# A hybrid layer's merge, output projection and Strassen quarters: whole row tiles, four banks at a time, one quarter summed on TensorE

## The chip, the cores and the metric

The kernel runs on one core of one Trainium2 chip. Its engines are TensorE (PE, with PEld for its weight loads), VectorE (DVE), ScalarE (ACT), GpSimd (POOL) and SyncE (SP, which only issues DMAs here). The metric is the device time of one execution in microseconds. Before the change it is 1715.71 us, the median of 3 runs (1714.04 to 1716.68).

## The reference

One layer of a hybrid decoder, 1024 tokens of width 1024 behind 16 meta tokens, all in float32:

```python
xn = rmsnorm(h, norm_mix)
q, k, v, u, g_att, g_ssm = jnp.split(xn @ w_in, offs, axis=-1)
attn = sliding_window_attention(rmsnorm(q), rmsnorm(k), v, attn_sinks)
y = s5_ssm(u, ...)                                   # diagonal complex scan
z = jax.nn.gelu(y)
za, zb = jnp.split(z @ w_glu, 2, axis=-1)
ssm = za * jax.nn.sigmoid(zb)
merged = (jax.nn.sigmoid(g_att) * rmsnorm(attn, attn_branch_norm)
          + jax.nn.sigmoid(g_ssm) * rmsnorm(ssm, ssm_branch_norm))
h = h + merged @ w_out
gate, up = jnp.split(rmsnorm(h, norm_ffn) @ w_ffn_in, 2, axis=-1)
h = h + (jax.nn.silu(gate) * up) @ w_ffn_out
```

## The kernel before

Every large product works on operands in two parts. `split` makes them: ScalarE casts the source to the TensorE format (`hi`), VectorE subtracts that from the source (`lo`), and the product is three passes, hi by hi, lo by hi and hi by lo, so a 128x512 output block over a depth of 1024 is 24 matmuls (`mm3`).

The work comes in stages. First the input projections, the state space scan and attention, up to about 680 us of the profiled execution. Then the scan's output y is made, passed through gelu, transposed, and split into four quarters of z (b11, t3, b21, b22), in the loop over `blk` whose helper is `z_turn`. The product with w_glu is a Strassen scheme of 2x2 quarters: seven products, with the keys "11", "12", "2", "3", "22", "1", "4", need three mixed quarters more, t2 = t3 + b11, t4 = b21 - t2 and t1 = b22 - t2. `mixed` makes those on VectorE. A unit is one such product for a pair of column blocks; its 12 matmuls a key go to PSUM banks named ch, si, th and ex. The first two units, (1,0) and (0,0), run together (`glu_step`), then the others follow.

Behind the gate comes the merge, `merge(h)`, once for each half of the tokens. It turns the sum of squares of ssm (a matmul, `ssq`) into a factor (14 small VectorE instructions), spreads it over partitions (a matmul, `rsb`, copied by ScalarE to `rs`), multiplies the eight blocks of ssm by it (L1055), adds the attention half, read back from DRAM in eight loads of 256 KB into cells `mpa` on SP's queue, and splits the sum into `mt`. The output projection then makes h = x + merged @ w_out in two column halves n and eight row blocks b (banks `wo`, evicted by VectorE in L1140 together with a load of x, `xr`), and norms and transposes h for the feed-forward part, which again is a Strassen product. There too t2, t4 and t1 are mixed, for the first two units (names with `_e`).

SBUF is handed out by pools of tiles. `pool_a` has 8 half tiles of 128 x 4 x 512 (class `Rows` joins two), `pool_x` holds the mixed quarters, `big` the pages, `mp` the cells. PSUM has 8 banks: tags m and s with 2 each, taken in turn, x with 3 and q with 1. The order of instructions on an engine is not that of the source: a scheduler places them by its own estimates, and each engine then runs its queue in order.

## Time and profile before

| | |
|---|---|
| median of 3 runs | 1715.71 us |
| the profiled execution | 1708.9 us, span 1707.1 us |
| PE busy | 1572.0 us, 92% of the span |
| DVE busy | 1262.4 us, 74% |
| ACT busy | 730.5 us, 43% |
| POOL busy | 296.5 us, 17% |
| mean granted clock of TensorE | 0.967 of full speed |

The profiled execution is one run with the profiler on; it is 6.8 us below the median. TensorE works almost without gaps over the whole span, except in a few short stretches. A stretch loses time in two ways: TensorE sits idle, which the timeline shows with the engine that released it, or its granted clock is below 1.00, which is the lower of its two levels for part of the stretch, and each matmul then takes longer though it counts as busy.

### The profile page before, as it was taken

The numbers are of one execution on the slowest core, as the hardware profiler recorded it, in microseconds if no ns is written. First come the engines' busy times: TensorE is split into PE (matmuls) and PEld (weight loads), VectorE is DVE, ScalarE is ACT, GpSimd is POOL, SyncE is SP. The second block draws the span as 40 slices with busy tenths as digits, with TensorE's granted clock in tenths as the row PEclk, the third lists the DMA queues.
The fourth block names the chain that finished last, engine by engine and source line by source line (L and its number), as shares of the span: only waits on it lengthen the run. The fifth ranks groups of instructions, "written<-read, shape, count | busy, mean of one in ns | idle before, by whom it ended". The sixth has DMA issues, their size and how long they took to land. (4 is left out here: it accounts for less than half of the span.)

```text
span 1707.1 us, 22184 instructions
## 1 busy us (share of the span) xinstructions
PE 1572.0 (92%) x7906; PEld 1299.7 (76%) x7906; DVE 1262.4 (74%) x2446; ACT 730.5 (43%) x1435; POOL 296.5 (17%) x233
## 2 busy tenths in 40 slices
PE   7999978989989999889996697999999999799998
PEld 5788868778867788857885585788888888678887
DVE  7779886999994799688756478966655656299763
ACT  4434425878985321554432233533333333243330
POOL 1001313333321000000000000111111112256441
PEclk9999989999999999989998898999999999899999
DMA  6254442011013763711234251323323331485431
GB/s 189 61 129 134 146 142 73 11 41 42 22 50 116 255 207 115 223 44 68 80 99 130 80 191 62 129 94 109 108 80 106 99 120 60 152 324 183 154 111 74
DMA packets 167166, 196.92 MB, mean 115 GB/s; under 512 B 12768, under 2 KB 117216, under 8 KB 166928
## 3 DMA queue, kind: packets, MB, share of 16 engines
q1 hardware_dynamic: 158544, 183.94, 33.2%
q10 hardware_dynamic: 8288, 11.01, 2.0%
q8 instruction: 62, 1.02, 0.3%
q0 software_dynamic: 224, 0.56, 0.1%
q14 instruction: 48, 0.39, 0.1%
HBM read 140.62 MB, written 54.85 MB: 115 GB/s over the span
## 5 line engine op out<-in xcount | busy, mean ns | idle before, releaser
L122 PE MATMUL g<-xn,wh_g 128*128 128x512 f32 x512 | 165.4, 404 | 1.3 <-ACT sg L548 1.2
L814 PE MATMUL ch<-B,A 128*128 128x512 f32 x528 | 126.5, 396 | 9.8 <-ACT B L1360 7.6
L814 PEld LDWEIGHTS ch<-B,A 128*128 128x128 f32 x528 | 100.2, 191 | 33.6 <-ACT B L1360 8.1
L122 PEld LDWEIGHTS g<-xn,wh_g 128*128 128x128 f32 x512 | 97.1, 192 | 24.6 <-ACT sg L548 2.1
L122 PE MATMUL q<-wh_q,xn 128*128 128x256 f32 x512 | 104.3, 291 | 4.2 <-ACT qp L620 4.2
L122 PE MATMUL wo<-wh_o,mt 128*128 128x512 f32 x256 | 84.0, 407 | 22.5 <-DVE h L1140 14.7
L122 PE MATMUL g<-xn,wl_g 128*128 128x512 f32 x256 | 102.6, 401 | 0.0
L818 POOL TENSOR_TENSOR a<-c_e,c_e 128x512 f32<-128x512 f32 x1 | 1.5, 1542 | 571.6 <-DVE c_e L818 571.6
L814 PE MATMUL si<-B,A 128*128 128x512 f32 x396 | 92.7, 389 | 0.0
L122 PE MATMUL u<-xn,wh_u 128*128 128x272 f32 (+2 forms) x384 | 91.7, 332 | 0.0
L122 PEld LDWEIGHTS q<-wh_q,xn 128*128 128x128 f32 x512 | 84.4, 195 | 5.8 <-ACT qp L620 4.6
L814 PEld LDWEIGHTS si<-B,A 128*128 128x128 f32 x396 | 74.3, 188 | 15.7 <-DVE h2o L818 0.3
L1360 ACT CAST A<-rawa 128x1536 fp32r<-128x1536 f32 (+1 forms) x28 | 38.5, 1374 | 96.3 <-issue 44.8
L122 PEld LDWEIGHTS wo<-wh_o,mt 128*128 128x128 f32 x256 | 50.0, 196 | 34.2 <-issue 15.1
L122 PE MATMUL q<-wl_q,xn 128*128 128x256 f32 x256 | 74.2, 290 | 0.0
L818 DVE TENSOR_TENSOR A<-rawa,A 128x1536 fp32r<-128x1536 f32 (+1 forms) x28 | 62.8, 2243 | 12.8 <-ACT A L1360 12.8
L669 ACT ACTIVATE pr<-pr,mn 128x272 f32<-128x272 f32 (+1 forms) x128 | 64.9, 507 | 16.5 <-DVE mn L663 14.0
L818 POOL TENSOR_TENSOR a<-c,c_fg 128x512 f32<-128x512 f32 x10 | 15.9, 1586 | 316.1 <-DVE c L818 211.1
L122 PEld LDWEIGHTS u<-xn,wh_u 128*128 128x128 f32 x384 | 66.1, 196 | 5.5
L818 POOL TENSOR_TENSOR B<-t,B 128x1536 fp32r<-128x1536 f32 (+1 forms) x16 | 60.3, 3781 | 50.5 <-ACT B L1360 50.5
L122 PE MATMUL u<-xn,wl_u 128*128 128x272 f32 (+2 forms) x192 | 63.0, 330 | 0.0
L818 DVE TENSOR_TENSOR h2o<-h2o,ch 128x512 f32<-128x512 f32 x64 | 42.3, 679 | 26.4 <-PE ch L814 24.3
(449 smaller groups left out, 4222.3 us busy)
## 6 DMA issues: line engine op xcount, KB each, us to landing
rawa<-act_d SPq DMA_DIRECT2D x21, 768.0 KB
raw_fg<-in_w_ffn_in_dram SPq DMA_DIRECT2D x20, 512.0 KB
raw_fu<-in_w_ffn_in_dram SPq DMA_DIRECT2D x20, 512.0 KB
rawb<-in_w_ffn_out_dram SPq DMA_DIRECT2D x6, 1536.0 KB
act_d<-a SPq DMA_DIRECT2D x33, 256.0 KB
raw_g<-in_w_in_dram SPq DMA_DIRECT2D x16, 512.0 KB
raw_z<-in_w_glu_dram SPq DMA_DIRECT2D x16, 512.0 KB
act_d<-c_fg SPq DMA_DIRECT2D x30, 256.0 KB
```

What stands on the lines that cost most here:

```text
L122: nc.tensor.matmul(o, lhs(kb, a), rhs(kb, b), start=(kb == 0 and i == 0), stop=(kb == n - 1 and i == 2))
L669: nc.scalar.activation(out=pr[:, h, :n], in_=pr[:, h, :n], func=AF.Exp, scale=-1.0, bias=mn[:, h:h + 1], accum_out=den[:, h:h + 1])
L814: nc.tensor.matmul(o, lhs(kb, a), rhs(kb, b), start=(first and kb == 0 and i == 0), stop=(kb == n - 1 and i == 2), skip_group_check=not first)
L818: eng.tensor_tensor(out=out, in0=in0, in1=in1, op=op)
L1360: nc.scalar.copy(hi, src)
```

## The change

It has six parts. (1) `pool_a` gets 4 whole row tiles of 128 x 8 x 512 in place of 8 halves, and the class `Rows` goes. (2) The quarters of z lie in pairs in such tiles, (b11, t3) and (b21, b22), so one split of 512 columns serves a transposed bank where two of 256 did; of four copies to `ss` per block VectorE makes two instead of three. (3) The first operands of the gate unit (1,0), for keys "11", "12" and "22", are made ahead of the loop over y. (4) The quarter t2 is summed on TensorE: four matmuls by an identity (`one_r`) add the hi and lo parts of t3 and b11 in one bank, ScalarE and VectorE split that bank, and ScalarE copies it out for the two other mixed quarters. In the FFN the sum stands ahead of both first units. (5) The attention half comes in four loads of 1 MB on GpSimd's queue, into tiles of `pool_x` that t2 and t1 leave free, and the merge adds in place in ssm. (6) The output projection's first column half works on four banks at once, one 128-deep slice after the other through all four.

```diff
-    pool_a = front.enter_context(sbuf("pool_a", 8))
+    pool_a = front.enter_context(sbuf("pool_a", 4))
+    one_r = const.tile([P, P], F32R, name="one_r")
+    nc.vector.tensor_copy(one_r, ident)
-    def mm3(o, lhs, rhs, n):
-        for kb in range(n):
+    def mm3(o, lhs, rhs, n, only=None):
+        for kb in range(n) if only is None else [only]:
...
+    def rows_a(name, n=512):
+        return pool_a.tile([P, KB, n], F32R, tag="a", name=name)
...
+    def x_pair(key):
+        t = rows_a(f"X{key}")
+        X[key] = [t[:, 4 * p:4 * p + 4, :] for p in range(2)]
...
-    def mixed(key, a, b, op):
+    def mixed(key, a, b, op, tag="s"):
+        if key == "t2":
+            for k in range(4):
+                pt = bank(f"{key}_{k}", tag)
+                for i, v in enumerate((X[b][0], X[b][1], X[a][0], X[a][1])):
+                    nc.tensor.matmul(pt, one_r, v[:, k, :], start=(i == 0), stop=(i == 3))
+                if k % 2 == 0:
+                    full[k] = page(f"{key}f{k}").rearrange("p (k n) -> p k n", k=2)
+                split(X[key][0][:, k, :], X[key][1][:, k, :], pt)
+                nc.scalar.copy(full[k // 2 * 2][:, k % 2, :], pt)
+            return
         for k in (0, 2):
             t = page(f"{key}f{k}").rearrange("p (k n) -> p k n", k=2)
...
-            if key == "t2":
-                full[k] = t
-                l2 = page(f"{key}l{k}").rearrange("p (k n) -> p k n", k=2)
-                tt_(t, hi, X[b][0][:, k:k + 2, :].bitcast(F32), op)
-                tt_(l2, lo, X[b][1][:, k:k + 2, :].bitcast(F32), op)
-                tt_(t, t, l2, ALU.add)
...
+    two = ((1, 0), (0, 0))
+    a2, ops = {two[0]: glu_raw(*two[0])}, {u: {} for u in two}
+    ops[two[0]] = glu_operands(a2[two[0]], ("11", "12", "22"), "10")
...
-            for h in range(2):
-                dst = [X[keys[h]][p][:, blk % 4].rearrange("p (n t) -> p t n", t=T)[:, 4 * i:4 * i + 4, :]
-                       for p in range(2)]
-                split(dst[0], dst[1], pt.rearrange("p (t n) -> p t n", t=4)[:, :, 64 * h:64 * h + 64])
+            dst = [Z[keys][p].rearrange("p (h k) (n t) -> p k t h n", h=2, t=T)[:, blk % 4, 4 * i:4 * i + 4]
+                   for p in range(2)]
+            split(dst[0], dst[1], pt.rearrange("p (t h n) -> p t h n", t=4, h=2))
...
-                cp_ = nc.vector.tensor_copy if e or ri else nc.scalar.copy
+                cp_ = nc.vector.tensor_copy if e else nc.scalar.copy
...
+        def load_pa(h):
+            pa[h] = [x_tile(f"pa{h}{i}").bitcast(F32) for i in range(2)]
+            for i in range(2):
+                nc.gpsimd.dma_start(out=pa[h][i], in_=pa_d[4 * i:4 * i + 4, :, 512 * h:512 * h + 512]
+                                    .rearrange("f p n -> p f n"))
 
         def merge(h):
             rs = rstd_cols(acc[h], 4, f"ssm{h}", mp, cell(f"rs{h}"))
             for f in range(KB):
                 src = ssm[h, f // 2][:, (f % 2) * 512:(f % 2) * 512 + 512]
-                pa = cell(f"mpa{f}{h}")
-                nc.sync.dma_start(out=pa, in_=pa_d[f][:, 512 * h:512 * h + 512])
                 nc.vector.tensor_tensor(out=src, in0=src, in1=rs, op=ALU.mult)
-                tt_(pa, pa, src, ALU.add)
-                split(mt[h][0][:, f, 0:512], mt[h][1][:, f, 0:512], pa)
+                tt_(src, src, pa[h][f // 4][:, f % 4, :], ALU.add)
+                split(mt[h][0][:, f, 0:512], mt[h][1][:, f, 0:512], src)
...
-                o = bank(f"wo{n}{b}")
-                mm3(o, lambda kb, part: mt[b // 4][part][:, kb, (b % 4) * P:(b % 4 + 1) * P], w, KB)
+                if n == 0 and b % 4 == 0:
+                    wo = [bank(f"wo{n}{b + i}") for i in range(4)]
+                    for kb in range(KB):
+                        for i in range(4):
+                            mm3(wo[i], lambda k, part: mt[b // 4][part][:, k, i * P:i * P + P], w, KB, kb)
+                o = wo[b % 4] if n == 0 else bank(f"wo{n}{b}")
...
         for key in ("t2", "t1", "t4"):
-            x_part(key, pool_a)
+            x_pair(key)
+        mixed("t2", "t3", "b11", ALU.add, "x")
```

The queues change at three places. First VectorE at the merge of the first half of the tokens: gs is the gate's factor of one of the last ssm blocks, rs the norm's factor, `mpa` and `pa` the attention half. Before:

```order
L1055 TENSOR_TENSOR ssm_8633<-ssm_8633,rs_8972 128x512 x2
L1055 TENSOR_TENSOR ssm_8887<-ssm_8887,rs_8972 128x512 x2
L818 TENSOR_TENSOR mpa_9003<-mpa_9003,ssm_7931 128x512
L818 TENSOR_TENSOR mpa_9009<-mpa_9009,ssm_7931 128x512
L818 TENSOR_TENSOR mpa_9015<-mpa_9015,ssm_8351 128x512
L818 TENSOR_TENSOR mpa_9021<-mpa_9021,ssm_8351 128x512
L818 TENSOR_TENSOR mpa_9027<-mpa_9027,ssm_8633 128x512
L818 TENSOR_TENSOR mpa_9033<-mpa_9033,ssm_8633 128x512
L200 TENSOR_TENSOR mt_0_8970<-mpa_9003,mt_0_8968 128x512
```

After, from the last small instruction of the norm:

```order
L148 SCALAR_TENSOR_TENSOR rs_i_ssm_8971<-rs_q_ssm_8970,rs_i_ssm_8971 128x4
L976 SCALAR_TENSOR_TENSOR ssm_8869<-ssm_8869,gates,gs_8947 128x512
L1072 TENSOR_TENSOR ssm_7890<-ssm_7890,rs_8960 128x512 x2
L1072 TENSOR_TENSOR ssm_8333<-ssm_8333,rs_8960 128x512 x2
L1072 TENSOR_TENSOR ssm_8615<-ssm_8615,rs_8960 128x512 x2
L1072 TENSOR_TENSOR ssm_8869<-ssm_8869,rs_8960 128x512 x2
L807 TENSOR_TENSOR ssm_8870<-ch_z_8866,zb_9049 128x512
L807 TENSOR_TENSOR ssm_7890<-ssm_7890,pa_8950 128x512
L807 TENSOR_TENSOR acc_8157<-acc_8157,sq_9065 128x512
```

The adds now read the large `pa` tiles and write ssm itself. The multiplication by gs, which stood ahead of the norm's chain, stands behind it, and the second half's last product with its gate and a sum of its squares stand among the adds.

Second TensorE at the start of the output projection: `wo` are the banks, `wh_o`, `wl_o` the two parts of w_out, `mt` the merged operand, `ssq_ssm` and `rsb_ssm` the norm's matmuls. Before:

```order
L748 MATMUL ssq_ssm_8973<-ones,acc_7960 128x1 x4
L757 MATMUL rsb_ssm_8997<-ident,rs_i_ssm_8983 128x128 x4
L122 MATMUL wo_9271<-wh_o_0_9216,mt_0_8968 128x512
L122 MATMUL wo_9271<-wl_o_0_9217,mt_0_8968 128x512
L122 MATMUL wo_9301<-wh_o_0_9216,mt_0_8968 128x512
L122 MATMUL wo_9301<-wl_o_0_9217,mt_0_8968 128x512
L122 MATMUL wo_9271<-wh_o_0_9216,mt_0_8970 128x512
L122 MATMUL wo_9271<-wh_o_0_9216,mt_0_8968 128x512
L122 MATMUL wo_9271<-wl_o_0_9217,mt_0_8968 128x512
```

After:

```order
L737 MATMUL ssq_ssm_8961<-ones,acc_7919 128x1 x4
L746 MATMUL rsb_ssm_8985<-ident,rs_i_ssm_8971 128x128 x4
L124 MATMUL wo_9195<-wh_o_0_9170,mt_8958 128x512
L124 MATMUL wo_9195<-wl_o_0_9171,mt_8958 128x512
L124 MATMUL wo_9196<-wh_o_0_9170,mt_8958 128x512
L124 MATMUL wo_9196<-wl_o_0_9171,mt_8958 128x512
L124 MATMUL wo_9197<-wh_o_0_9170,mt_8958 128x512
L124 MATMUL wo_9197<-wl_o_0_9171,mt_8958 128x512
L124 MATMUL wo_9198<-wh_o_0_9170,mt_8958 128x512
L124 MATMUL wo_9198<-wl_o_0_9171,mt_8958 128x512
L737 MATMUL ssq_ssm_9093<-ones,acc_8157 128x1 x4
L124 MATMUL wo_9195<-wh_o_0_9170,mt_8959 128x512
```

Eight matmuls with the hi part of the first slice now run through four banks, the second half's sum of squares comes right behind them, and from there all else waits for the first lo part. Before, that sum of squares stood behind 51 of the matmuls and its `rsb` behind 84; now they stand behind 8 and 53.

Third VectorE where the first two FFN units are prepared. `nt_h` are transposed blocks of h, `Xt3`, `Xb11`, `Xb22` the quarters, t2f and t2l the sums for t2, `sf` and `wf` operands of w_ffn_in. Before:

```order
L818 TENSOR_TENSOR sf3_0_10091<-raw_f00_10082 128x512
L200 TENSOR_TENSOR Xt31_9751<-nt_h7_t3_10006,Xt30_9750 128x4x128
L818 TENSOR_TENSOR t2f0_10123<-Xt30_9750,Xb110_9208 128x1024
L200 TENSOR_TENSOR Xb221_9213<-nt_h7_b22_10013,Xb220_9212 128x4x128
L818 TENSOR_TENSOR t2l0_10124<-Xt31_9751,Xb111_9209 128x1024
L818 TENSOR_TENSOR t2f2_10130<-Xt30_9750,Xb110_9208 128x1024
L818 TENSOR_TENSOR t2l2_10131<-Xt31_9751,Xb111_9209 128x1024
L200 TENSOR_TENSOR wf03_10093<-sf3_0_10091,wf03_10093 128x512
L200 TENSOR_TENSOR wf04_10096<-sf4_0_10087,wf04_10096 128x512
L200 TENSOR_TENSOR wf02_10137<-sf0_10086,wf02_10137 128x512
```

After:

```order
L189 TENSOR_TENSOR Xb221_9167<-nt_h7_b22_9966,Xb220_9166 128x4x128
L189 TENSOR_TENSOR Xt2_10025<-t2_0_10028,Xt2_10025 128x512
L189 TENSOR_TENSOR Xt2_10025<-t2_1_10037,Xt2_10025 128x512
L189 TENSOR_TENSOR Xt2_10025<-t2_2_10045,Xt2_10025 128x512
L807 TENSOR_TENSOR sf0_10070<-raw_f00_10066,raw_f01_10068 128x512
L189 TENSOR_TENSOR Xt2_10025<-t2_3_10054,Xt2_10025 128x512
L807 TENSOR_TENSOR sf0_10070<-sf0_10070,raw_f00_10066 128x512
L807 TENSOR_TENSOR sf4_0_10071<-raw_f01_10068,sf0_10070 128x512
L807 TENSOR_TENSOR sf3_0_10075<-raw_f00_10066 128x512
L189 TENSOR_TENSOR wf03_10077<-sf3_0_10075,wf03_10077 128x512
```

The sums for t2 are gone from VectorE's queue, four short subtractions stand for them, and the sums for `sf0`, `sf3` and `sf4`, which came among the transposes, stand behind these.

## Rows read from the trace of the kernel before

**Rows 1.** Windows of stages: length, each engine's busy us (instructions), clock, DMA share, GB/s.

```profile
700.00:730.00 30.00, 25.64 (x201) 23.41 (x199) 19.32 (x34) 18.07 (x36) 0.00 (x0) 1.00 0.64 187
730.00:760.00 30.00, 24.08 (x97) 17.97 (x98) 23.77 (x34) 17.07 (x30) 0.00 (x0) 0.89 0.19 62
760.00:780.00 20.00, 15.51 (x51) 11.17 (x51) 20.00 (x20) 7.68 (x9) 0.00 (x0) 0.83 0.00 1
895.00:985.00 90.00, 60.62 (x255) 48.99 (x254) 50.61 (x99) 22.45 (x42) 0.00 (x0) 0.81 0.34 108
1050.00:1080.00 30.00, 17.49 (x54) 12.97 (x55) 30.00 (x35) 13.70 (x20) 0.00 (x0) 0.74 0.13 41
1082.00:1707.00 625.00, 608.69 (x2659) 499.08 (x2657) 408.06 (x482) 212.80 (x300) 173.47 (x72) 0.99 0.37 129
```

**Rows 2.** Timeline of TensorE, first gate units: start, us, group [idle before, releaser].

```profile
731.52 1.50 PE L863 MATMUL zT<-ident,z 128*128 128x128 f32 x12 [0.83 <-DVE z L818]
...
740.49 4.98 PE L814 MATMUL ch_z<-Xb,wz 128*128 128x512 f32 x12 [2.39 <-ACT wz L199]
...
762.00 4.05 PE L814 MATMUL si_z<-Xb,wz 128*128 128x512 f32 x10 [1.45 <-DVE wz L200]
...
775.03 0.88 PE L814 MATMUL ch_z<-Xt,wz 128*128 128x512 f32 x2 [2.04 <-ACT Xt L199]
```

**Rows 3.** Timeline of ScalarE, the same stretch.

```profile
738.00 1.28 ACT L954 ACT_TABLE_LOAD   x1
...
739.83 3.20 ACT L199 CAST wz<-raw_z 128x512 fp32r<-128x512 f32 x6
```

**Rows 4.** Timeline of VectorE, z's quarters and the first gate units.

```profile
699.52 1.16 DVE L200 TENSOR_TENSOR Xb<-zT,Xb 128x256 fp32r<-128x256 f32 x2 [0.91 <-ACT Xb L199]
...
754.98 1.22 DVE L818 TENSOR_TENSOR t2f<-Xt,Xb 128x1024 f32<-128x1024 f32 x1
...
759.52 0.69 DVE L200 TENSOR_TENSOR wz<-raw_z,wz 128x512 fp32r<-128x512 f32 x1
```

**Rows 5.** Timeline of TensorE, merge and output projection.

```profile
907.27 2.08 PE L757 MATMUL rsb_ssm<-ident,rs_i_ssm 128*128 128x128 f32 x8 [4.86 <-DVE rs_i_ssm L159]
916.21 0.80 PE L122 MATMUL wo<-wh_o,mt 128*128 128x512 f32 x1 [6.86 <-ACT mt L199]
...
931.38 0.95 PE L748 MATMUL ssq_ssm<-ones,acc 128*128 128x1 f32 x8
...
939.81 1.05 PE L757 MATMUL rsb_ssm<-ident,rs_i_ssm 128*128 128x128 f32 x8
...
958.32 0.77 PE L122 MATMUL wo<-wh_o,mt 128*128 128x512 f32 x1 [14.71 <-DVE h L1140]
```

**Rows 6.** Timeline of VectorE, merge and output projection.

```profile
902.89 0.75 DVE L966 SCALAR_TENSOR_TENSOR ssm<-ssm,gates,gs 128x512 f32<-128x512 f32 x1 [2.34 <-DMA gs<-sg_d]
...
910.00 4.90 DVE L1055 TENSOR_TENSOR ssm<-ssm,rs 128x512 f32<-128x512 f32 x8 [2.79 <-ACT rs L759]
914.83 3.69 DVE L818 TENSOR_TENSOR mpa<-mpa,ssm 128x512 f32<-128x512 f32 x6
...
941.57 4.90 DVE L1055 TENSOR_TENSOR ssm<-ssm,rs 128x512 f32<-128x512 f32 x8 [6.66 <-ACT rs L759]
...
957.49 0.69 DVE L1140 TENSOR_TENSOR h<-wo,xr 128x512 f32<-128x512 f32 x1 [0.60 <-DMA xr<-in_x_dram]
```

**Rows 7.** Timeline of TensorE, first FFN units.

```profile
1064.60 1.22 PE L814 MATMUL th_e<-Xt,wf 128*128 128x512 f32 x2 [6.03 <-ACT wf L199]
...
1077.68 3.03 PE L814 MATMUL ch_e<-Xt,wf 128*128 128x512 f32 x12 [2.80 <-ACT c_e L1233]
```

**Rows 8.** Timeline of VectorE, first FFN units.

```profile
1045.91 0.69 DVE L200 TENSOR_TENSOR Xt<-nt_h_t,Xt 128x512 fp32r<-128x512 f32 x1
```

**Rows 9.** DMA issues on GpSimd's queue: KB each, us from issue to landing.

```profile
kl_d<-zrows POOLq DMA_DIRECT2D x1, 448.0 KB, 3.4
lt<-in_lam_re_dram POOLq DMA_DIRECT2D x1, 32.0 KB, 6.5
```

More of the change, by code (lines that the diff above doesn't have):

```diff
@@ L855, in hybrid_layer_kernel, with glu_raw @@
-    for key in ("b11", "t3", "b21", "b22"):
-        x_part(key, pool_a)
+            tt_(t, hi, full[k], op)
+            tt_(t, t, lo, ALU.add)
+            split(X[key][0][:, k:k + 2, :], X[key][1][:, k:k + 2, :], t)
+    def glu_raw(which, j, in_pages=False):
+        a = {}
+        for i in range(2):
+            t = page(f"raw_z{which}{j}{i}") if in_pages else pool_r.tile([P, 1024], F32, tag="raw",
+                                                                         name=f"raw_z{which}{j}{i}")
+            t = t.rearrange("p (k n) -> p k n", k=4)
+            c0 = which * D + 2 * j * P
+            nc.sync.dma_start(out=t, in_=w_glu[i * 512:(i + 1) * 512, c0:c0 + 256]
+                              .rearrange("(k p) n -> p k n", p=P))
+            for n in range(2):
+                a[f"{n + 1}{i + 1}"] = t[:, :, n * P:n * P + P]
+        return a
@@ new lines, in glu_operands @@
+    def glu_operands(a, keys, name):
+        ops = {}
+        for key in keys:
+            if key == "2":
+                tt_(a["22"], a["21"], a["22"], ALU.add)
+                tt_(a["21"], a["11"], a["21"], ALU.subtract)
+                tt_(a["11"], a["22"], a["11"], ALU.subtract)
+                tt_(a["12"], a["12"], a["11"], ALU.subtract)
+                a |= {"1": a["22"], "3": a["21"], "2": a["11"], "4": a["12"]}
+            ops[key] = parts_of(pool_w.tile([P, 2, 512], F32R, tag="w", name=f"wz{key}_{name}"))
+            split(*ops[key], a[key])
+        return ops
@@ L857, in hybrid_layer_kernel, with z_pair @@
+    two = ((1, 0), (0, 0))
+    a2, ops = {two[0]: glu_raw(*two[0])}, {u: {} for u in two}
+    ops[two[0]] = glu_operands(a2[two[0]], ("11", "12", "22"), "10")
+    def z_pair(p, keys):
+        t = rows_a(f"Z{keys[0]}{p}")
+        for i, key in enumerate(keys):
+            X.setdefault(key, []).append(t[:, 4 * i:4 * i + 4, :])
+        return t
+    Z = {keys: [z_pair(p, keys) for p in range(2)] for keys in (("b11", "t3"), ("b21", "b22"))}
     zs = {}
@@ L1020, in glu_banks, with prepare @@
                 banks[u]["4"] = bank(f"ex_z{u[0]}{u[1]}", apart)
[L1023 to L1030 removed]
+        ua, ub = two
+        a2[ub] = glu_raw(*ub, in_pages=True)
+        def prepare(u, *keys):
+            ops[u] |= glu_operands(a2[u], keys, f"{u[0]}{u[1]}")
+        prepare(ub, "11", "12")
         for u in two:
@@ L1070, in hybrid_layer_kernel @@
         for h in range(2):
-            mt[h] = [Rows(f"mt{h}{p}") for p in range(2)]
+            if h == 0:
+                for i in range(2):
+                    load_pa(i)
+            mt[h] = [rows_a(f"mt{h}{p}") for p in range(2)]
             merge(h)
```

93 lines of the change are left out of this document (27 added, 66 removed).

## The prediction

> **What bounds the kernel now.** I read the windows of the stages first, then the timelines of TensorE inside the windows that lose time, and for each gap there the engine that is named as its releaser. The windows say where something can be won [rows 1]. From 1082 us on TensorE is busy 608.69 of 625 us at a clock of 0.99; 2659 matmuls in that time make 0.229 us for each, which I use for a matmul at full clock. Four windows lose more. Making z (700 to 730): 4.4 us idle. First gate units (730 to 780): 10.4 us idle, and the lower clock costs about 24.1 x 0.11 + 15.5 x 0.17 = 5.3 us more, 15.7 us in all; VectorE is busy 20.00 of the last 20 us. Merge and projection (895 to 985): 29.4 us idle, with a clock of 0.81. First FFN units (1050 to 1080): 12.5 us idle, 17.5 x 0.26 = 4.5 us by the clock, and VectorE is busy 30.00 of 30 us. The change touches just these four. Elsewhere its reordered rows meet a TensorE that hardly waits; I give that 0 with 1.5 us to either side.
>
> **Gate units and z (A).** Six sums of 128x1024 and two subtractions of that size leave VectorE for t2, 8 x 1.22 = 9.8 us [rows 4]; four subtractions of 128x512 come, 4 x 0.69 = 2.8 us. TensorE gets 16 matmuls, 16 x 0.229 = 3.7 us. ScalarE gives two casts of 1024 columns for eight instructions of 512, at about 0.53 us each (six casts in 3.20 us [rows 3]). It is busy 24.8 of these 50 us [rows 1], so its 2 us more hide, unless its order makes TensorE wait.
>
> That order I walked from the point where z's last block is ready, 731.52 [rows 2], with these durations. Before, 12 transposes there are followed by eight pairs of cast and subtraction, then by a table load of 1.28 us and six operand casts [rows 3], so that unit (0,0) starts at 740.49, 9.0 us later, at a low clock: 12 matmuls in 4.98 us. After, four casts and subtractions do, and keys "11" and "12" of unit (1,0) need nothing but z, since their operands are there. Those end about 4.1 us after the zero, the operand of (0,0) comes at 4.2, its lo part at 5.6 (a loss of 0.9), and from there TensorE has work: the t2 sums stand among matmuls that are ready, and the t4 and t1 subtractions come about as TensorE reaches them. I find gaps of some 2.0 us up to 4.2, then 0.9, then 0.7, and put 1.5 us for matmuls at the lower clock behind them; with the 3.7 us of sums that is 8.8 us where 15.7 were lost, a gain of 6.9. In z's window each splitting of 256 columns costs 0.58 us on VectorE [rows 4] where half of one of 512 would cost 0.35, and TensorE has matmuls of the gate to fill with; of the 4.4 us I take 1. So A is 8 us. Its bounds: 0, if the sums' wait for ScalarE takes back what the first 5 us give, and 13, if all the idle time but the sums goes.
>
> [...] The trace shows a subtraction of 128x512 from PSUM in 0.69 us [rows 8] and one from SBUF in 0.69 us [rows 4], so the place costs nothing here. [...]
>
> **Merge and projection (B).** Before, the norm's chain starts late since the multiplication by gs waits 2.34 us for its DMA at the queue's head [rows 6]; it now stands behind the chain, so `rsb`, at 907.27 [rows 5], comes some 2.3 us sooner and the eight multiplications run from about 907.6 instead of 910.00 [rows 6]. They take 4.9 us, so 912.5; the second half's last product with its gate, 913.1; seven adds at 0.61 (six in 3.69 us), and between them two sums of squares and a multiplication of 0.7, end at 919.7; the first lo part at 920.3; the last at 925.2.
>
> TensorE can start at about 914.4 with eight hi matmuls at the low clock, then the second half's sum of squares (input at 919.7), then waits for the first lo until about 920.7. From there 184 matmuls x 0.229 = 42.1 us, and 1.9 us of small matmuls. The second chain follows at once: its `ssq` is at about 921 instead of 931.38, its `rsb` 45 matmuls later, near 932 instead of 939.81 [rows 5], multiplications from 933.5 instead of 941.57 [rows 6], adds to 943.1, the first lo 943.7. Group one's matmuls end there too, at 943 to 944. The second group, which before waits 14.71 us and starts at 958.32 [rows 5], then starts at about 944.4 behind the first eviction. That eviction before stood at 957.49, behind `mt` and a load of x whose queue also carried the `mpa` loads [rows 6]; these are gone. The other three come between the lo's, at 947, 950 and 950.5, before their banks are needed. I get the end of the column half at 966.7, with 1.5 us for low clock. Before, 96 matmuls from 958.32 at 0.229 and about 2 us of low clock put it at 982.3. The difference is 15.6; I take 15. Bounds: 17, if the eight early matmuls raise the clock sooner, and 8, if group two still waits half its 14.7 us for the second half's lo parts.
>
> This needs the 1-MB loads in time. The first two may start when key "2" of the last unit has read t2, near 886, the other two near 897. Needed are they at 913.1, 916, 938 and 940.5. The nearest row is a store of 448 KB on the same queue, 3.4 us; in proportion 1 MB takes 7.8 us, one behind the other 894, 902, 910 and 918. A load of 32 KB took 6.5 us there [rows 9], so from above I take 6.5 + 7.8 = 14.3 us for the first, at 900. Hidden, then, with 13 to 19 us to spare. The cover is lost only when the first lands after 913, and from there each microsecond is one.
>
> **First FFN units (C).** The same 9.8 us of VectorE become 2.8 us. But the sums for `sf0`, `sf4` and `sf3`, which VectorE made earlier in its idle time, now stand behind t2: four at 0.69, 2.8 us. And TensorE's 3.7 us of sums run in its gap. Walked from the last transposes, the second unit's first operand comes at 1063.1 instead of 1064.60 and its matmuls are as slow as before (two in 1.22 us); the step whose start ends the gap at 1077.68 [rows 7] waits for ScalarE's eviction, and I find that at 1075.5. C is 2.2 us, taken as 2.5 with the better clock; bounds 0 (ScalarE's order) and 8 (the gap's 7 us of VectorE come back in full, and clock).
>
> **Sum.** 8 + 15 + 2.5 = 25.5 us against the profiled execution, 1708.9 us, which gives 1683.4; that is 6.8 us under the median, and I apply the difference to the median: 1715.7 - 25.5 = 1690.2, so 1690.
>
> **Rivals.**
> *The second half gates again.* Group two waits for merge(1) because its chain, now with 53 matmuls ahead of `rsb` and an eviction among its lo's, comes late. For it: before, the same chain missed by 14.7 us. Against it: its `ssq` starts 10 us sooner. B is then 8, the sum 18.5: 1697.
> *The sums are paid and not won.* A and C give nothing: TensorE's queue is in order, and t2's banks come free only by ScalarE's copies, so what VectorE saves appears as waits for ScalarE. For it: gaps with ScalarE as releaser are there already (2.39 and 2.04 us [rows 2], 6.03 and 2.80 [rows 7]). Against it: it is idle half the time. 15 remain: 1701.
> *More than that.* The low clock goes with the gaps in all four stretches: A 12, B 17, C 6, 1681.
> *Slower: the loads on GpSimd's queue land late.* The multiplied blocks wait in the adds, and everything behind them in VectorE's queue with them. From a landing of the first at 913 on B shrinks, and at 913 + 25.5 = 938.6, 53 us after its issue, the kernel is no faster; at 945 it would take 1722. For it: the queue's small loads are its slow ones, 6.5 us for 32 KB [rows 9], and VectorE is full while the four are under way. Against it: it would need some four times the upper estimate. [...]
>
> **Chances.** Forecast (gain 19 to 31 us) 0.66; second half gates 0.11; sums not won 0.11; more than that 0.06; slower by late loads or nothing won 0.06. The range takes in the first two rivals and the favourable edge: 1681 to 1703. A difference of 0.2%, 3.4 us, is about what can be told from none. Faster 0.92, within it 0.03, slower 0.05.
>
> **What would show it.** In the profile after: no gap of over 3 us before a `wo` matmul from 925 on, and the step from n=0 to n=1 some 23 us earlier; `pa` loads landing in under 12 us; VectorE's adds without a wait for DMA; in the 50 us behind z's last block about 9 us lost, sums included, where 15.7 were; t2's subtractions at 0.69 us; VectorE still the fuller engine in C, and TensorE's gap there shorter by 2 to 3 us only. Wrong would be: TensorE waiting for ScalarE around `t2_` banks for more than 4 us in A, or a second gap of over 7 us in the projection.

## The result and the profile after

The changed kernel takes 1688.47 us, the median of 4 runs (1686.84 to 1688.96), against 1716.20 for 4 runs of the kernel before: a ratio of 0.9838, with a 95% interval of 0.9821 to 0.9855, or 27.7 us less. The forecast was 1690. Its profiled execution has a span of 1687.2 us where the other's was 1707.1, so the two profiles differ by 19.9 us only. To see where the difference lies I cut the span at the same instructions, in these two traces and in a second profile of the kernel before, whose span is 1715.8:

| stretch | before | before, second profile | after |
|---|---|---|---|
| start to y's first matmul | 683.0 | 689.1 | 683.4 |
| Z: from there to the first sum of squares of ssm | 218.5 | 218.5 | 207.8 |
| M: to the last transposes of h | 143.6 | 143.7 | 129.5 |
| F: to the FFN's second product | 441.4 | 443.0 | 440.5 |
| S: the second product, to the end | 220.6 | 221.4 | 226.0 |

Z holds the prediction's term A, M its B, F its C. Together they are 803.5 us before and 777.8 after, 25.7 us less. The stretch ahead of them, which the change hardly touches, took between 680.2 and 689.6 us in fourteen profiles of this study, and S between 220.2 and 226.9. S, 5.4 us longer after, and the start take 5.8 us of that back, which leaves the 19.9. The other 8 lie in the first profile of the kernel before, which ran 7.3 us under its median; the second reached Z 6.1 us later. So the stretches are what I compare below, with the medians beside them.

The windows of the trace after, moved to the same places of the work as in [rows 1] (columns: window, length, busy us and instructions of TensorE, its weight loads, VectorE, ScalarE and GpSimd, clock, DMA share, GB/s):

```profile
698.40:728.40 30.00, 28.14 (x227) 26.40 (x225) 18.76 (x22) 22.30 (x32) 0.00 (x0) 1.00 0.74 213
728.40:758.40 30.00, 26.76 (x109) 20.32 (x108) 21.78 (x31) 18.44 (x29) 0.00 (x0) 0.89 0.23 79
758.40:778.40 20.00, 20.00 (x90) 16.55 (x89) 19.11 (x23) 9.92 (x15) 0.00 (x0) 1.00 0.00 1
884.80:974.80 90.00, 75.98 (x323) 61.91 (x322) 56.69 (x120) 26.98 (x49) 0.02 (x1) 0.89 0.39 131
1024.60:1054.60 30.00, 20.32 (x63) 14.84 (x63) 28.91 (x38) 16.51 (x27) 0.00 (x0) 0.77 0.19 56
```

In the third window TensorE has no gap and a clock of 1.00, where it was busy 15.51 of 20 us at 0.83. In the fourth it does 323 matmuls where it did 255. In the last its clock is 0.77, hardly above the 0.74 of before, and VectorE is still full.

TensorE in the gate units (start, duration, group, idle before and its releaser), for [rows 2]:

```profile
729.88 1.50 PE L901 MATMUL zT<-ident,z 128*128 128x128 f32 x12 [0.61 <-DVE z L807]
732.60 0.50 PE L803 MATMUL ch_z<-Zb,wz 128*128 128x512 f32 x1 [1.22 <-ACT Zb L188]
...
736.90 1.06 PE L803 MATMUL ch_z<-Zb,wz 128*128 128x512 f32 x2
738.54 2.93 PE L803 MATMUL ch_z<-Zb,wz 128*128 128x512 f32 x6 [0.58 <-DVE wz L189]
```

And VectorE ahead of the step at 738.54:

```profile
737.20 0.69 DVE L807 TENSOR_TENSOR zc<-zc,si_z 128x512 f32<-128x512 f32 x1 [1.37 <-PE si_z L803]
737.80 0.68 DVE L189 TENSOR_TENSOR wz<-raw_z,wz 128x512 fp32r<-128x512 f32 x1
```

Behind 738.54 TensorE waits nowhere for more than 0.3 us until the first sum of squares; before, it waited 0.75, 1.45, 0.70, 2.04 and, close to the end of the gate, 2.06 us. But unit (0,0) begins 7.0 us behind the start of those transposes, with two matmuls at 736.90, and goes on at 738.54, 8.66 us behind, when the lo part of its operand is there; I had walked 4.2 and 5.6 us. (The expectation of a run below gives 8.7 us for the unit's start; that is its third matmul.)

TensorE and VectorE at the merge, for [rows 5] and [rows 6]:

```profile
895.25 2.08 PE L746 MATMUL rsb_ssm<-ident,rs_i_ssm 128*128 128x128 f32 x8 [2.96 <-DVE rs_i_ssm L148]
904.79 0.80 PE L124 MATMUL wo<-wh_o,mt 128*128 128x512 f32 x1 [7.46 <-ACT mt L188]
...
910.22 1.05 PE L737 MATMUL ssq_ssm<-ones,acc 128*128 128x1 f32 x8 [1.65 <-DVE acc L807]
...
923.07 1.05 PE L746 MATMUL rsb_ssm<-ident,rs_i_ssm 128*128 128x128 f32 x8
...
935.85 0.64 PE L124 MATMUL wo<-wh_o,mt 128*128 128x512 f32 x1 [1.95 <-DVE h L1167]
```

```profile
896.12 0.75 DVE L976 SCALAR_TENSOR_TENSOR ssm<-ssm,gates,gs 128x512 f32<-128x512 f32 x1 [0.93 <-DMA gs<-sg_d]
897.98 4.90 DVE L1072 TENSOR_TENSOR ssm<-ssm,rs 128x512 f32<-128x512 f32 x8 [1.10 <-ACT rs L748]
...
903.40 0.68 DVE L807 TENSOR_TENSOR ssm<-ssm,pa 128x512 f32<-128x512 f32 x1
904.00 0.68 DVE L807 TENSOR_TENSOR acc<-acc,sq 128x512 f32<-128x512 f32 x1
...
909.48 0.68 DVE L807 TENSOR_TENSOR acc<-acc,sq 128x512 f32<-128x512 f32 x1
```

The second half's `ssq` now follows the first by 19.0 us where 29.9 lay between them, because its two sums of squares (`acc`) run among the first half's additions. The wait of 14.71 us ahead of the second group of `wo` [rows 5] is 1.95. The 1-MB loads of pa land in 8.6 us (issues of the queue: KB each, median us to landing), and no addition waits for one:

```profile
pa<-pa_d POOLq DMA_DIRECT2D x4, 1024.0 KB, 8.6
```

TensorE at the first FFN units, for [rows 7]:

```profile
1030.08 1.22 PE L803 MATMUL th_e<-Xt,wf 128*128 128x512 f32 x2 [3.98 <-ACT wf L188]
...
1052.31 3.02 PE L803 MATMUL ch_e<-Xt,wf 128*128 128x512 f32 x12 [1.88 <-ACT c_e L1259]
```

The gap of 6.03 us has become 3.98, but 3.7 us of sums for t2 stand ahead of it, and at 1052.31 the kernel is 25.4 us ahead of [rows 7], where it was 24.4 ahead at the last transposes of h.

S holds the same instructions before and after, yet in the trace after TensorE waits 3.79 us for VectorE once, and its gaps over 0.5 us there sum to 14.5 where they were 9.0. Here are that wait, VectorE ahead of it, and GpSimd beside it:

```profile
1509.51 2.90 PE L803 MATMUL ch<-B,A 128*128 128x512 f32 x6 [3.79 <-DVE h2o L807]
```

```profile
1494.75 1.75 DVE L807 TENSOR_TENSOR A<-rawa,A 128x1536 fp32r<-128x1536 f32 x1
1496.42 5.05 DVE L807 TENSOR_TENSOR t<-rawb 128x1536 f32<-128x1536 f32 x1
...
1503.18 4.40 DVE L807 TENSOR_TENSOR A<-rawa,A 128x1536 fp32r<-128x1536 f32 x1
```

```profile
1494.92 4.93 POOL L807 TENSOR_TENSOR B<-rawb,B 128x1536 fp32r<-128x1536 f32 x1 [1.41 <-ACT B L1386]
1502.45 3.51 POOL L807 TENSOR_TENSOR B<-rawb,B 128x1536 fp32r<-128x1536 f32 x1 [2.60 <-ACT B L1386]
```

The same VectorE instruction takes 1.75 us or 4.40, and the next `h2o` additions, for which TensorE waits, stand behind the long ones. Each of the two long ones begins while one of GpSimd is under way and ends 1.62 us behind it (1499.85 and 1501.47, 1505.96 and 1507.58), as if it had begun only then. It is so all through S in the two traces: of the 33 of this size on VectorE in each, those that begin while one of GpSimd's is under way, 11 before and 10 after, end 1.61 to 1.62 us behind it, and the others take 1.74 to 1.76. The additions to `h2o`, with one input in PSUM, stay at 0.67 to 0.69 us, also the 46 of the trace after that run wholly beside one of GpSimd's. The kernel before has such long instructions as well: in S, 9 of the 33 last over 3 us in either trace, and all 33 together take 79.9 us before and 81.3 after. So the change did not bring them; they can only fall in other places.

### The profile page after: what moved, and what is told of

Same layout as the page of the kernel before. It is cut to its first block, busy times and chain, and to the rows that moved or that the text cites. A ratio compares the mean times of both kernels' runs of the same rounds, so it can differ in the third digit from the quotient of the medians.

```text
span 1687.2 us, 22176 instructions
## 1 busy us (share of the span) xinstructions
PE 1577.3 (93%) x7938; PEld 1304.0 (77%) x7938; DVE 1251.0 (74%) x2415; ACT 738.6 (44%) x1439; POOL 295.6 (18%) x237
## 4 chain that ended last, share of the span: by engine, by line
PE 52%; DVE 18%; DMA 7%; issue 4%; ACT 3%; SPq 0%; ACTq 0%; DVEq 0%
PE ch_fg L803 6%; PE ch_fu L803 6%; PE wo L124 5%; PE ch L803 4%; PE ch_z L803 4%; PE th_fg L803 3%; PE th_fu L803 3%; PE si L803 3%; PE th_z L803 2%; PE q L124 2%; DVE pr L652 2%; PE si_fg L803 2%; PE si_fu L803 2%; PE g L124 1%; DVE A L807 1%
## 5 line engine op out<-in xcount | busy, mean ns | idle before, releaser
L807 DVE TENSOR_TENSOR A<-rawa,A 128x1536 fp32r<-128x1536 f32 (+1 forms) x28 | 69.2, 2472 | 13.0 <-ACT A L1386 13.0
```

The lines of the kernel that those rows point to most:

```text
L807: eng.tensor_tensor(out=out, in0=in0, in1=in1, op=op)
```

## Experiments

Each is the changed kernel with the edit that is shown, except the second profile of the kernel before. The stretches of all profiles, in us, with the median of the timed runs and its ratio to the kernel before (95% interval); medians of before in these comparisons were 1713.5 to 1714.3. The changed kernel itself was timed only beside a before of 1716.2, so a median below can be compared with its 1688.5 to some 2 us:

| kernel | Z | M | F | S | median | ratio |
|---|---|---|---|---|---|---|
| before, second profile | 218.5 | 143.7 | 443.0 | 221.4 | | |
| after | 207.8 | 129.5 | 440.5 | 226.0 | 1688.5 | 0.982 to 0.986 |
| merge and projection undone | 206.8 | 140.4 | 441.7 | 226.9 | 1701.8 | 0.991 to 0.995 |
| projection bank by bank | 205.1 | 127.9 | 441.8 | 222.4 | 1686.9 | 0.983 to 0.988 |
| pa by cells | 207.4 | 140.2 | 441.4 | 220.9 | 1696.5 | 0.988 to 0.992 |
| gate's t2 on VectorE | 210.8 | 133.0 | 441.2 | 221.3 | 1693.5 | 0.987 to 0.990 |
| operands not made ahead | 207.8 | 129.5 | 440.3 | 226.1 | 1689.5 | 0.984 to 0.988 |
| z split by halves | 210.7 | 127.7 | 442.6 | 220.8 | 1692.4 | 0.986 to 0.989 |
| FFN's t2 on VectorE | 206.9 | 127.9 | 446.9 | 221.2 | 1692.6 | 0.987 to 0.991 |
| z, four elements innermost | 202.4 | 130.5 | 440.2 | 226.2 | 1687.6 | 0.983 to 0.986 |
| FFN's sums first | 207.5 | 129.7 | 438.2 | 221.4 | 1682.9 | 0.980 to 0.983 |
| gate undone | 221.2 | 127.7 | 442.3 | 220.2 | 1697.5 | 0.989 to 0.992 |
| four innermost and sums first | 204.2 | 129.6 | 438.0 | 221.2 | 1680.0 | 0.977 to 0.981 |

Where the projection and what feeds it stay as in the changed kernel, M lies between 127.7 and 130.5 with one exception at 133.0 (the gate's t2 on VectorE, where `rsb` stands 5.8 us behind the first sum of squares and not 4.0); differences under 3 us there I don't read.

### Merge and projection undone

```diff
...
+                pa = cell(f"mpa{f}{h}")
+                nc.sync.dma_start(out=pa, in_=pa_d[f][:, 512 * h:512 * h + 512])
                 nc.vector.tensor_tensor(out=src, in0=src, in1=rs, op=ALU.mult)
-                tt_(src, src, pa[h][f // 4][:, f % 4, :], ALU.add)
-                split(mt[h][0][:, f, 0:512], mt[h][1][:, f, 0:512], src)
+                tt_(pa, pa, src, ALU.add)
+                split(mt[h][0][:, f, 0:512], mt[h][1][:, f, 0:512], pa)
...
-                if n == 0 and b % 4 == 0:
...
+                o = bank(f"wo{n}{b}")
+                mm3(o, lambda kb, part: mt[b // 4][part][:, kb, (b % 4) * P:(b % 4 + 1) * P], w, KB)
```

> The changed kernel with the merge and the output projection as they were before: pa's tiles loaded one by one on SP's queue into cells, and the eight banks of n = 0 one after the other. Theory 1 (term B of the prediction, 15 us, was won here and by these two edits): about 15 us longer than the changed kernel's 1688.5, 1703 (1699 to 1706), with the two waits for the merge in front of a wo bank back. Rival (the projection was only pulled along by the shorter gate stage ahead of it, the two edits did little): at most 5 us longer, 1688 to 1693.

1701.8, and M grew by 10.9 us while Z did not. Theory 1 holds: the projection's gain was won here and not upstream. Not all of it came back; M is still 3.2 us shorter than before. One us of that is seen in the trace: `rsb` stands 4.8 us behind the first sum of squares, and 5.8 before, since the multiplication by gs, ahead of the norm's chain again, waits 0.1 us here and not 2.3 [rows 6]. The rest stays open.

### Projection bank by bank

The second half of that diff alone.

> The changed kernel with its early loads of pa, but the eight banks of n = 0 one after the other again. Theory 1 (both edits share B): the first bank of the first half can't end before the last row's low part, about 917 in the trace after, and three banks of 5.2 us follow, so that half ends near 932.5 where it ended near 926: 6 us; the second half's last low part is there at 942 and it ends 1 us later; together 7 us longer, 1695.5 (1692.5 to 1698). Rival (with pa there early, the rows come as fast as one bank uses them): 0 to 2 us, 1688.5 to 1690.5.

1686.9, and M is 127.9: the rival. Undoing the sixth part of the change costs nothing. The order in which the scheduler placed the matmuls says why: although each bank is written as one loop, they run through four banks in turn. Eight with the hi part come first and then the second half's sum of squares, as in the changed kernel; only behind that the order differs, with three matmuls a bank here. TensorE's queue in this kernel, from the merge on (banks 9195, 9225, 9255 and 9285):

```
L746 MATMUL rsb_ssm_8985<-ident,rs_i_ssm_8971 128x128 x4
L124 MATMUL wo_9195<-wh_o_0_9170,mt_8958 128x512
L124 MATMUL wo_9195<-wl_o_0_9171,mt_8958 128x512
L124 MATMUL wo_9225<-wh_o_0_9170,mt_8958 128x512
L124 MATMUL wo_9225<-wl_o_0_9171,mt_8958 128x512
L124 MATMUL wo_9255<-wh_o_0_9170,mt_8958 128x512
L124 MATMUL wo_9255<-wl_o_0_9171,mt_8958 128x512
L124 MATMUL wo_9285<-wh_o_0_9170,mt_8958 128x512
L124 MATMUL wo_9285<-wl_o_0_9171,mt_8958 128x512
L737 MATMUL ssq_ssm_9093<-ones,acc_8157 128x1 x4
```

And the waits come out alike:

```profile
909.56 1.05 PE L737 MATMUL ssq_ssm<-ones,acc 128*128 128x1 f32 x8 [1.84 <-DVE acc L807]
...
935.17 0.47 PE L124 MATMUL wo<-wh_o,mt 128*128 128x512 f32 x1 [1.95 <-DVE h L1160]
```

### pa by cells

The first half of that diff alone: rows in order, pa in eight 256-KB loads a half.

> The changed kernel with the projection by rows, but pa's tiles loaded one by one on SP's queue into cells that also hold the gates. Theory 1 (both edits share B, and by-banks costs 7 of 15): about 8 us longer, 1696.5 (1693.5 to 1699.5), with VectorE's additions waiting for DMAs. Rival (the order by rows alone does it, since rows come in order at any pace): under 3 us, 1688.5 to 1691.5.

1696.5, and M is 140.2, as long as with both undone. So this edit alone carries it: pa loaded early, into tiles of its own. The reason that I gave was wrong, though: VectorE sits idle ahead of none of these additions. VectorE, and then TensorE:

```profile
907.67 3.69 DVE L807 TENSOR_TENSOR mpa<-mpa,ssm 128x512 f32<-128x512 f32 x6
911.28 0.69 DVE L189 TENSOR_TENSOR mt<-mpa,mt 128x512 fp32r<-128x512 f32 x1
...
912.48 3.70 DVE L189 TENSOR_TENSOR mt<-mpa,mt 128x512 fp32r<-128x512 f32 x6
...
917.29 0.69 DVE L807 TENSOR_TENSOR acc<-acc,sq 128x512 f32<-128x512 f32 x1
...
919.16 0.69 DVE L807 TENSOR_TENSOR acc<-acc,sq 128x512 f32<-128x512 f32 x1
```

```profile
909.06 0.79 PE L124 MATMUL wo<-wh_o,mt 128*128 128x512 f32 x1 [6.87 <-ACT mt L188]
...
950.83 0.77 PE L124 MATMUL wo<-wh_o,mt 128*128 128x512 f32 x1 [13.79 <-DVE h L1158]
```

The second `acc` starts 19.1 us behind the first `rsb` (900.11) where it was 14.2 in the kernel after, at the end of the first half's additions and lo parts and not among them, and the second half's `ssq` (924.58) 24.5 us behind it against 15.0. From there that half's chain is late, and 13.79 us of waiting are back.

What holds it up is the cells. Pool `mp` has seven of them, and not only `mpa` but also `rs`, gs, and the second half's gate `zb` and squares `sq` lie in them. The loads on SP's queue, and ScalarE:

```profile
897.24 3.14 SPq L1065 DMA_DIRECT2D mpa<-pa_d  x6
...
907.83 4.49 SPq L1065 DMA_DIRECT2D mpa<-pa_d  x2
914.40 1.52 SPq L975 DMA_DIRECT2D gs<-sg_d  x2
```

```profile
913.20 0.60 ACT L964 ACTIVATE zb<-ch_z 128x512 f32<-128x512 f32 x1
913.81 0.63 ACT L969 ACTIVATE sq<-ssm 128x512 f32<-128x512 f32 x1
```

Beside `rs`, six loads find a cell. The seventh is issued at 907.83, as the last multiplication by `rs` ends (907.76), the eighth at 911.99, as the first lo part (911.28 and 0.69 us) frees the first `mpa`. The next cell comes free when the second lo part ends, 0.69 us behind 912.48, and then, at 913.20, `zb` is made, 13.1 us behind `rsb`; `sq` (913.81) and a load of gs (914.40) follow as the next two lo parts end. In the kernel after, where pa has its own tiles, `zb` comes 2.6 us behind `rsb`:

```profile
897.84 0.60 ACT L964 ACTIVATE zb<-ch_z 128x512 f32<-128x512 f32 x1
```

So the tiles of its own count, since they leave the cells to the second half; no run gave `mp` more cells, or loaded pa late into its own tiles, so what either would bring alone is not shown.

### The kernel before again

> The kernel before once more, for a second profile of its last stage, the feed-forward block's second product, which the change leaves as it was (from the start of its first operands' product 220.6 us in the trace before, 225.9 in the trace after). Theory 1 (that stage's length varies from run to run with how VectorE's and GpSimd's operand work fall on one another): this run's stage differs from 220.6 by over 2 us. Rival (the change lengthened it): 220.6 within 1 us again.

S took 221.4, within 1 us of the first profile, so theory 1 fails for this kernel. All the same it is not settled that the change lengthened S: of the nine profiles in which VectorE's queue there stands in the order of the kernel after, five took 220.8 to 222.4 and four 226.0 to 226.9; of the five with the order of the kernel before, all took 220.2 to 221.4. Z and M agree with the first profile within 0.1 us, and the start differs by 6.1.

### Gate's t2 on VectorE

```diff
-        if key == "t2":
+        if key == "t2" and tag == "x":
             for k in range(4):
...
+        if key == "t2":
+            for k in (0, 2):
+                full[k] = t = page(f"{key}f{k}").rearrange("p (k n) -> p k n", k=2)
+                l2 = page(f"{key}l{k}").rearrange("p (k n) -> p k n", k=2)
+                hi, lo = (X[a][p][:, k:k + 2, :].bitcast(F32) for p in range(2))
+                tt_(t, hi, X[b][0][:, k:k + 2, :].bitcast(F32), op)
+                tt_(l2, lo, X[b][1][:, k:k + 2, :].bitcast(F32), op)
+                tt_(t, t, l2, ALU.add)
+                split(X[key][0][:, k:k + 2, :], X[key][1][:, k:k + 2, :], t)
...
```

> The changed kernel with t2 of the gate units summed on VectorE again, at the place where TensorE sums it now; the FFN's t2 stays on TensorE. Read on one stretch, from the last group of z's transposes to the first sum of squares of ssm: 166.4 us in both profiles of the kernel before, 156.3 to 158.4 in four profiles with the changed gate stage. Theory 1 (A was won by the 9.8 us of sums that leave VectorE, less 2.8 and 3.7): about 4 us longer, 161 to 165, and the total 1691 to 1695. Rival (A was won by the operands made ahead): under 2 us, at most 160, total 1687 to 1690.

The stretch from z's last transposes is 162.5 and the total 1693.5, both inside theory 1. Waits for a mixed quarter (`Xt`) are back at two steps, the one that needs t2 and a later one; TensorE:

```profile
750.15 0.51 PE L803 MATMUL ch_z<-Xt,wz 128*128 128x512 f32 x1 [1.67 <-ACT Xt L188]
...
769.98 0.73 PE L803 MATMUL ch_z<-Xt,wz 128*128 128x512 f32 x2 [1.53 <-ACT Xt L188]
```

### Operands not made ahead

```diff
-    a2, ops = {two[0]: glu_raw(*two[0])}, {u: {} for u in two}
-    ops[two[0]] = glu_operands(a2[two[0]], ("11", "12", "22"), "10")
...
+        for u in two:
+            prepare(u, "11", "12", "22")
...
```

> The changed kernel without the operands made ahead: those of unit (1,0) are cast with those of (0,0) behind the loop over y, as before. Theory 1 (VectorE's sums carry A, the operands little, since unit (0,0) starts 8.7 us behind the zero after the change as it did 9.0 before): stretch from z's last transposes to the first sum of squares 158 to 161, total 1687 to 1691. Rival (prediction's walk: the operands bring the first 4 to 5 us of A): 162 to 164, total 1692 to 1695.

158.1 us from z's last transposes, Z the same 207.8, and 1689.5: theory 1. Alone this edit is worth nothing that can be told.

### z split by halves

```diff
...
-            split(dst[0], dst[1], pt.rearrange("p (t h n) -> p t h n", t=4, h=2))
+            for h in range(2):
...
+                split(dst[0], dst[1], pt.rearrange("p (t n) -> p t n", t=4)[:, :, 64 * h:64 * h + 64])
```

> The changed kernel with z's quarters still in paired tiles, but each transposed bank split by two casts and two subtractions of 256 columns instead of one of 512. Theory 1 (the paired cast and subtraction took 1.13 and 1.11 us in the trace after, where two of 256 took 1.1 to 1.3 together): the stretch from y's first matmul to z's last transposes, 52.1 before and 48.4 to 49.5 since, stays within 1 us, and the total within 2, 1686.5 to 1690.5. Rival (prediction: one instruction of 512 costs 0.7, so the pairs save 0.23 us a half on either engine): 1 to 3 us longer there and in the first gate units, total 1690 to 1693.

52.3 us from y's first matmul to z's last transposes, as before, and 1692.4: theory 1, which I had formed from the trace after, falls. The rival's range holds, but not the prediction's price behind it: one instruction of 512 takes 1.1 us and not 0.7, so a pair saves less than I had. The instructions in this kernel, and in the one after (min/median/max ns):

```profile
L188 ACT CAST Zb<-zT x32: 616/652/810, 706.0 to 743.9; 128x256 fp32r<-128x256 f32 x32
L189 DVE TENSOR_TENSOR Zb<-zT,Zb x32: 596/626/699, 706.7 to 744.5; 128x256 fp32r<-128x256 f32 x32
```

```profile
L188 ACT CAST Zb<-zT x16: 1089/1119/1272, 700.0 to 733.6; 128x512 fp32r<-128x512 f32 x16
L189 DVE TENSOR_TENSOR Zb<-zT,Zb x16: 1076/1096/1241, 701.2 to 734.7; 128x512 fp32r<-128x512 f32 x16
```

A pair saves 2 x 652 - 1119 = 185 ns on ScalarE and 156 on VectorE; sixteen of them save 3.0 and 2.5 us, and Z is 2.9 us longer without them.

### FFN's t2 on VectorE

The same code as for the gate, with the tags exchanged.

> The changed kernel with the FFN's t2 summed on VectorE, still ahead of both first units; the gate's t2 stays on TensorE. Read from the last transposes of h to the start of the FFN's second product, 441.4 and 443.0 us before, 440.5 to 441.8 since. Theory 1 (C is nearly nothing with the sum on TensorE, because sf0, sf4 and sf3 now stand behind t2 in VectorE's queue; on VectorE at this same early place it is worse still): 3 to 8 us longer, 444 to 449, total 1691 to 1696. Rival (VectorE's sums would have hidden here too): within 1.5 us, total 1687 to 1690.

F is 446.9 and the total 1692.6: theory 1. With VectorE full (no wait from 1019.73 until behind that step), sums of 1.22 us each and the sums for the first operands go through one queue, and one wait takes it all:

```profile
1035.55 1.22 PE L803 MATMUL th_e<-Xt,wf 128*128 128x512 f32 x2 [16.04 <-ACT wf L188]
```

### z, four elements innermost

```diff
-            dst = [Z[keys][p].rearrange("p (h k) (n t) -> p k t h n", h=2, t=T)[:, blk % 4, 4 * i:4 * i + 4]
+            dst = [Z[keys][p].rearrange("p (h k) (n t) -> p k h n t", h=2, t=T)[:, blk % 4, :, :, 4 * i:4 * i + 4]
                    for p in range(2)]
-            split(dst[0], dst[1], pt.rearrange("p (t h n) -> p t h n", t=4, h=2))
+            split(dst[0], dst[1], pt.rearrange("p (t h n) -> p h n t", t=4, h=2))
```

> The changed kernel with one thing in the split of z's transposed banks changed: the axes of the two instructions are walked in another order, so that four neighbouring elements are written innermost where 64 elements 32 bytes apart were; what is written where, and the order of all instructions, stays. In the trace after, this cast of 128x512 took 1.13 us and the subtraction 1.11 us, where a subtraction of 128x512 with plain operands took 0.69. Theory 1 (the wide step of the writes costs the 0.4 us): cast and subtraction fall to 0.7 to 0.85, the stretch from y's first matmul to the first sum of squares, 205.1 to 207.8 us with the changed gate stage so far, gets 1 to 4 us shorter, total 1684 to 1688. Rival (the cost is in the number of short runs or in reading the bank, not in the step of the writes): 1.1 us or more each, the stretch 206 to 212, total 1688 to 1693.

```profile
L188 ACT CAST Zb<-zT x16: 585/592/623, 704.5 to 734.0; 128x512 fp32r<-128x512 f32 x16
L189 DVE TENSOR_TENSOR Zb<-zT,Zb x16: 679/690/692, 705.1 to 734.6; 128x512 fp32r<-128x512 f32 x16
```

Theory 1: both instructions fall to the time of plain ones, and Z by 5.4 us (by 2.7 to 5.4 against all kernels with the gate as changed). Only the order in which the two instructions walk the elements differs: 64 elements 32 bytes apart innermost at 1119 and 1096 ns, four neighbours at 592 and 690. Why that order counts, no run shows. The total of 1687.6 is only 0.9 us lower, inside the spread of the runs; in this kernel's profile S is 226.2. The lo part that came 8.66 us behind the transposes in the kernel after comes 6.3 us behind them here (they start at 731.28):

```profile
737.55 2.56 PE L803 MATMUL ch_z<-Zb,wz 128*128 128x512 f32 x10 [0.98 <-DVE wz L189]
```

### FFN's sums first

```diff
-        mixed("t2", "t3", "b11", ALU.add, "x")
         for u in range(2):
             banks[u] |= {"3": bank(f"th_e{u}", "x"), "4": bank(f"ex_e{u}", "q" if u else "x")}
...
             first_operands(u, ("3", "4"), quarters[u], sums[u])
+            if u == 0:
+                mixed("t2", "t3", "b11", ALU.add, "x")
```

> The changed kernel with the sums sf0, sf4 and sf3 of the first FFN unit ahead of t2's subtractions in VectorE's queue again, t2 still summed on TensorE. Read from the last transposes of h to the start of the FFN's second product: 441.4 and 443.0 us before, 440.5 to 441.8 after. Theory 1 (C gave only some 1 us because these sums, made in VectorE's idle time before, stand behind t2 now): 437 to 439, total 1685 to 1687.5. Rival (ScalarE's casts or the slower clock bound that stretch whatever VectorE does): 440 to 442, total 1687 to 1690.

F is 438.2, a gain of 2.3 us, and the median of 1682.9 lies below the range of theory 1, so F is not all of it; S is 221.4 here, with VectorE's queue there in the order of the kernel before. VectorE makes the sums among h's last transposes, and ScalarE casts them at 1022.75 where it was 1029.41 in the trace after. VectorE, then ScalarE, of this kernel:

```profile
1019.10 0.68 DVE L807 TENSOR_TENSOR sf<-raw_f,sf 128x512 f32<-128x512 f32 x1
...
1021.79 0.69 DVE L807 TENSOR_TENSOR sf<-raw_f 128x512 f32<-128x512 f32 x1 [0.21 <-PE nt_h_t L1133]
```

```profile
1022.75 1.67 ACT L188 CAST wf<-sf 128x512 fp32r<-128x512 f32 x3
```

### Gate undone

The edits of three experiments together: t2 on VectorE, no operands ahead, z by halves.

> The changed kernel with its three edits in the gate stage undone together: z's banks split by halves of 256, t2 summed on VectorE, operands of unit (1,0) cast behind the loop over y. One by one, undoing them made the stretch from y's first matmul to the first sum of squares 210.7, 210.8 and 207.8 us long, where it is 205.1 to 207.8 with all three and 218.5 in both profiles before. Theory 1 (the three are A and cover for each other in part): 215 to 219, total 1696 to 1701. Rival (they add up, and the rest of the 11 us comes from elsewhere, such as the multiplication by gs that was moved): 213 to 215, total 1693 to 1696.

1697.5, inside theory 1's range, and Z at 221.2 is beyond both: 13.4 us more than after, where the three alone cost 3.0, 0 and 2.9 (kernels that leave the gate as changed have a Z of 205.1 to 207.8). So they cover for each other: with one of them undone the other two still feed TensorE, and with all undone it waits again at several steps, 0.6 to 3.7 us each; the longest:

```profile
773.83 1.22 PE L803 MATMUL th_z<-Xt,wz 128*128 128x512 f32 x2 [3.65 <-ACT Xt L188]
```

Z is 2.7 us longer than in the kernel before; t2 stands at the changed kernel's place in the code here, ahead of the second operands, and that may be why.

### Four innermost and sums first

> The changed kernel with both edits that shortened a stage: z's banks split with four neighbouring elements innermost, and the sums sf0, sf4, sf3 ahead of t2's subtractions. Alone they made the stretch from y's first matmul to the first sum of squares 202.4 us (205.1 to 207.8 otherwise) and that from h's last transposes to the second product 438.2 (440.5 to 441.8 otherwise), yet the totals came out at 1687.6 and 1682.9. Theory 1 (stages add up, and the total of the first was lost in the second product, which took 226.2 us in its profile where others took 220 to 222): both stretches as alone, total 1676 to 1681. Rival (what the earlier stage gains is taken back behind it every time): total 1681.5 to 1685.

1680.0 (1674.7 to 1680.9), a ratio of 0.9792 (0.9773 to 0.9810): theory 1, and 8.5 us less than the changed kernel, the best version here. Its Z gains 3.6 us on the changed kernel's, F 2.5, and S is 221.2.

## Why the prediction came out right, and where it did not

The sum was 25.5 us; Z, M and F together give 25.7. By terms it was 8, 15 and 2.5, and the profiles give 10.7, 14.1 and 0.9 to 2.5 (against the first and the second profile of before). That the sums agree so closely is in part luck: A came out 2.7 us above its term, B and C up to 2.5 below theirs, and S was 5.4 us longer, which no term had, while the profile of before from which I reckoned lay under its median.

**A: the size near, one step of the walk wrong.** The step that failed is the one by which unit (0,0)'s operand comes 4.2 us and its lo part 5.6 us behind the zero, because z's last block needs only four casts and subtractions. The matmuls that need them began 7.0 and 8.66 us behind it. I priced the four at what a plain instruction of 512 columns costs, half of which "would cost 0.35"; they took 1.12 and 1.10 us. With four neighbours innermost they take 0.59 and 0.69 us, about what I had priced, and the lo part came 6.3 us behind the zero: that price is 2.4 of the 3.1 us. My own rows held the warning: [rows 4] has 0.58 us for 256 columns of z, and elsewhere 0.69 for 512 and 1.22 for 1024. A straight line through the last two, an estimate, has 0.16 us at no columns and about 0.42 for 256 plain ones, not 0.58. In the 50 us behind z's last block 3.2 us of idle time, 26.76 x 0.11 = 2.9 of low clock and 3.7 of sums were lost, 9.8 where I had 8.8, a gain of 5.9; what was missing came where I had taken little or nothing: z's own window is 2.5 us fuller (28.14 busy of 30, 25.64 before [rows 1]), and a wait of 2.06 us for VectorE at the end of the gate is gone. Undone alone, t2 on TensorE costs 3.0 us in Z, the pairs 2.9, and the operands ahead, to which the walk owed its first 5 us, nothing; undone together the three cost 13.4.

**B: right in size; of the two parts that the walk rests on, one carries it.** Its walk left A out, so 10.2 us, the shift of the first sum of squares, are to be taken off its times: `ssq` 911 (came at 910.22), `rsb` 922 (923.07), second group 934.2 (935.85), end of the column half 956.5 (959.3). The first `rsb` came 4.0 us behind its sum of squares, 5.8 before: 1.8 of the 2.3 us that I took for gs. The loads landed in 8.6 us, between the 7.8 and the 14.3 that I had. What I credited as well was the order by rows; it is the scheduler's order already for the first eight matmuls, and writing it out brings nothing. The runs give the gain to pa in tiles of its own, which lets the second half's squares run ahead because the seven cells are free for them. That the cells held these squares back before, the prediction did not see.

**C: the mechanism right, the size too large.** The sums behind t2 were priced at 2.8 us of VectorE; the gap in front of the first operand is still 3.98 us, with 3.7 us of TensorE's sums ahead of it. 2.5 was forecast, 0.9 to 2.5 measured, and with the sums ahead of t2 another 2.3 came.

**Elsewhere 0 +- 1.5** failed in the profile: S was 5.4 us longer. I had ruled out a cost because TensorE hardly waited there; but VectorE's queue stands in another order, and which of its additions stand behind an instruction that takes over 4 us beside one of GpSimd's can cost TensorE 3.79 us at once. Whether the new order does that is open: with it S took 220.8 to 222.4 us in five kernels and 226.0 to 226.9 in four.

**The rivals.** The second half did not gate again (1.95 us). The sums were not paid in vain: with ScalarE as releaser TensorE waits nowhere over 0.3 us around the gate's t2 banks. The loads were not late: they landed in 5.6 to 10.3 us, and VectorE was not full while they were under way but busy some 10 of 17 us. Nor was it more than that: no term reached the 12, 17 and 6 us of that rival.
